# A fixed order for the entry of a fp32 decoder trunk, rotary tables under the value columns, and more raw rooms for the memory projection

## The chip, the cores and the metric

The kernel runs on one core of a Trainium2 chip. The metric is the device time of one launch in microseconds. Engines are named as in the profile: PE (TensorE, matrix products), PEld (its weight loads), DVE (VectorE), ACT (ScalarE), POOL (GpSimd) and SP (SyncE, which issues most DMAs).

## The reference

Two layers over 1024 rows of width 1024, all in fp32. Layer 0 is attention in three groups of dilated windows, layer 1 a gated linear recurrence; each also attends to 256 memory rows. Cut to layer 0, where the change lies:

```
h = rms_norm(x, norm_gain[0])
cols = h @ w_in_a                      # 1024 x 11264: q, k, v of 3 groups, memory queries, gate
q, k = rms_norm(q, q_gain), rms_norm(k, k_gain)
q, k = apply_partial_rotary(q, cos, sin), apply_partial_rotary(k, cos, sin)   # first 32 of 128 columns of a head
mix  = dilated window attention of each group, merged by softmax denominators
kv   = rms_norm(mem, mem_gain) @ w_kv                 # for both layers
mem_out = softmax(rms_norm(q_mem) @ km.T) @ vm
y    = concat(mix, mem_out) * silu(gate)
x    = x + y @ w_out
```

`cos` and `sin` are tables of `positions * inv_freq`, 1024 rows by 16 frequencies.

## The kernel before

A product in fp32 is made of three matmuls: each operand is split into a high part and a low part (`hi`, `lo`; ACT copies the high part, DVE or POOL subtracts it), and hi x hi, hi x lo and lo x hi are added in PSUM. Weights come by DMA as raw pieces of 512 KB ("raw" rooms in SBUF), and ACT and DVE split them into `wh` and `wl` (four of each).

The program of layer 0, in order of time:

1. **The entry.** Eight row tiles of x (128 rows each) are loaded, normalized (ACT squares and sums a row, DVE and POOL make the inverse root `rv`, `rr`, DVE scales `xt`), turned by eight PE transposes a tile (`pt`, L857) and split into `hhi` and `hlo`. The tiles come in pairs, j and j + 4. Of each pair three block sums (`s2`, `s3`, `s4`, and `s1` in place) are made for the next stage. Under it runs the projection of the first 512 gate columns: per tile 8 x 3 matmuls (L286 to L288), 192 in all, then tanh, a product and a write to `gate_scr`. POOL also makes the rotary tables here. A scheduler sets the order of the instructions on each engine by its own costs.
2. **The column groups.** Nine groups of 1024 columns (q, k or v of one window group) by Strassen's seven products, so 28 steps of twelve matmuls a group (`step`, L995 to L997), in the order keys, values, queries for group 2. Queries and keys are normalized and rotated (POOL) and turned. Here the order on each engine is pinned as written.
3. **The memory part.** Keys and values of the memory for both layers (`mem_part`), with the raw pieces loaded into two rooms in turn (L198), then the 512 memory query columns (L1291 to L1293) and the attention to the memory. Keys are turned and written ("spilled") some steps after their product, from a list `later`, one entry at each query tile.
4. Attention of the three groups, output projection, layer 1.

`pinned(...)` adds ordering dependencies, so that an engine executes in the written order; without engines named it holds for PE alone.

Of the kernel before, what the change touches and what calls it, by code (L numbers as in the profile page):

```python
# [24 lines left out]
I32 = mybir.dt.int32  # L25
# [78 lines left out]
def trunk_kernel(ctx, tc, x, mem, pos, norm_gain, w_in_a, q_gain_a, k_gain_a, qk_gain_t, w_out_a,  # L104
# [89 lines left out]

    def piece_raw(src):

        raw = rpool.tile([128, 1024], F32, name="raw")
        WQ.dma_start(raw[:].rearrange("p (a b) -> p a b", a=src.shape[1]), src)  # L198
        return raw
# [459 lines left out]
    plan_chunk(("gate", 0), w_in_a, GATE_A)  # L659
# [108 lines left out]
    with ExitStack() as sa:  # L768
# [29 lines left out]
        def tables():  # L798

            posi = wx.tile([128, NT], I32, name="m2")  # L800
            Y.dma_start(posi[:], pos[:, 0:NT])
            flat = room("m3").rearrange("p h d -> p (h d)")
            n_ = NT * 16
            v3 = lambda o: flat[:, o:o + n_].rearrange("p (a b) -> p a b", b=16)
            ang, kk, tmp = v3(0), v3(n_), v3(2 * n_)
            inv, posf = flat[:, 3 * n_:3 * n_ + 16], flat[:, 3 * n_ + 16:3 * n_ + 16 + NT]
            G.tensor_copy(posf, posi[:])
            Y.dma_start(inv, cst[:, C_IF:C_IF + 16])
            n3 = [128, NT, 16]
            G.tensor_tensor(ang, bc(posf[:, :, None], n3), bc(inv[:, None, :], n3), op=OP.mult)  # L810
# [7 lines left out]
            for big in (4096.0, 1.0):  # L818
                G.tensor_scalar(kk, ang, 1.0 / (2.0 * math.pi * big), magic, op0=OP.mult, op1=OP.add)
                G.tensor_scalar(kk, kk, -magic, None, op0=OP.add)  # L820
                for c in parts:
                    G.tensor_scalar(tmp, kk, -c * big, None, op0=OP.mult)
                    G.tensor_tensor(ang, ang, tmp, op=OP.add)
            G.tensor_scalar(ang, ang, 3.1415925, -3.1415925, op0=OP.min, op1=OP.max)
            A.activation(sn, ang, AF.Sin)
            A.activation(cs, ang, AF.Sin, scale=0.5)
            G.tensor_tensor(cs, cs, cs, op=OP.mult)
            G.tensor_scalar(cs, cs, -2.0, 1.0, op0=OP.mult, op1=OP.add)
            for i, gn in enumerate((q_gain_a, k_gain_a)):
                Y.dma_start(gr[:, i], bass.AP(tensor=gn.tensor, offset=gn.offset, ap=[[0, 128], [HD, NG], [1, ROT]]))  # L830
            gt = wx.tile([128, 2 * NG], F32, name="m2")
            Y.dma_start(gt[:], qk_gain_t)
            V.tensor_tensor(gqk, gt[:, :NG], gt[:, NG:], op=OP.mult)
            V.memset(gqk[0:ROT, :], 1.0)
# [5 lines left out]
        s1raw = {}  # L840

        def x_pair(j):

            t_, r = {}, {}
            for half in range(2):
                m = j + 4 * half
                xt = ipool.tile([128, D], F32, name="xt", bufs=2)
                first = Y.dma_start(xt[:], tile_of(x, m))
                if m == 0:
                    with tc.issue_after(first.ins):  # L850
                        row_bcast(gain[:], norm_gain[0], D)
                        Y.dma_start(ident[:], cst[:, C_ID:C_ID + 128])
                norm_rows(xt[:], gain[:], D, ipool, bufs=1, inplace=True)
                for kh in range(2):
                    t = pT.tile([128, 4, 128], F32, name="pt")
                    for b in range(4):
                        T.transpose(t[:, b, :], xt[:, (4 * kh + b) * 128:(4 * kh + b + 1) * 128], ident[:])  # L857
                    hi, lo = (hts[n][:, 4 * kh:4 * kh + 4, m * 128:(m + 1) * 128] for n in ("hi", "lo"))
                    split_evac(hi, lo, t[:])
                    if (half, kh) != (1, 1):  # L860
                        r[half, kh] = ipool.tile([128, 4, 128], F32, name=f"r{half}{kh}")[:]
                        copy(A, r[half, kh], t[:])
                    else:
                        s1raw[j] = room(f"m{j}")
                        V.tensor_tensor(s1raw[j], r[1, 0], t[:], op=OP.add)
                if half:
                    for i, n in enumerate(("hi", "lo")):
                        Y.dma_start(a21_scr[i][:, :, j * 128:(j + 1) * 128], hts[n][:, 0:4, m * 128:(m + 1) * 128].bitcast(F32))
            at = slice(j * 128, (j + 1) * 128)

            def keep(s, src):
                copy(A, sums[s, "hi"][:, :, at], src)
                G.tensor_tensor(sums[s, "lo"][:, :, at], src, sums[s, "hi"][:, :, at].bitcast(F32), op=OP.subtract)

            c3 = room(f"u{j % 2}")
            V.tensor_tensor(c3, r[0, 0], r[1, 0], op=OP.subtract)
            keep("s3", c3)
            c2 = room(f"w{j % 2}")
            V.tensor_tensor(c2, s1raw[j], r[0, 0], op=OP.subtract)
            keep("s2", c2)  # L880
            c4 = room(f"u{(j + 1) % 2}")
            V.tensor_tensor(c4, r[0, 1], c2, op=OP.subtract)
            keep("s4", c4)
# [192 lines left out]
        def step(k, fill=None):  # L1076
# [771 lines left out]
```

## Time and profile before

| | |
|---|---|
| median of 3 runs | 2092.5 us (2089.14 to 2092.95) |
| the profiled execution | 2096.68 us |
| its span | 2094.8 us, granted clock 0.994 |
| PE busy | 2051.2 us, 98% |
| DVE, ACT, POOL busy | 58%, 41%, 26% |
| entry (0 to the first matmul of L995) | 80.75 us |
| DMA | 277.22 MB, mean 132 GB/s |

The span runs from the first to the last instruction of one profiled execution. "Busy" of PE counts pipelined matmuls whose ends are modelled. A row of the timeline has its start, its duration, engine, line, operation and tiles (out<-in), shape and type, count, and in brackets the idle time of the engine before it and what ended it.

### The profile page before, as it was taken

The numbers are of one execution on the slowest core, as the hardware profiler recorded it, in microseconds if no ns is written. First come the engines' busy times: TensorE is split into PE (matmuls) and PEld (weight loads), VectorE is DVE, ScalarE is ACT, GpSimd is POOL, SyncE is SP. The second block draws the span as 40 slices with busy tenths as digits, with TensorE's granted clock in tenths as the row PEclk, the third lists the DMA queues.
The fourth block names the chain that finished last, engine by engine and source line by source line (L and its number), as shares of the span: only waits on it lengthen the run. The fifth ranks groups of instructions, "written<-read, shape, count | busy, mean of one in ns | idle before, by whom it ended". The sixth has DMA issues, their size and how long they took to land.

```text
span 2094.8 us, 29661 instructions
## 1 busy us (share of the span) xinstructions
PE 2051.2 (98%) x10713; PEld 1732.8 (83%) x10713; DVE 1220.6 (58%) x2452; ACT 860.8 (41%) x1635; POOL 553.1 (26%) x701
## 2 busy tenths in 40 slices
PE   6999999999999999999899999999999999999999
PEld 5788888888888888788788888888888888888887
DVE  5665467746757357555567454425477663776443
ACT  6454355633654245446667332224432222222220
POOL 7363066703746036121123200013100000000221
PEclk9999999999999999999999999999999999999999
DMA  6368469553553425517998474331201211213642
GB/s 204 101 122 120 130 126 110 126 147 97 126 136 113 159 81 189 173 31 271 307 314 288 146 263 148 123 90 46 76 28 60 65 51 41 61 51 96 236 131 110
DMA packets 418898, 277.22 MB, mean 132 GB/s; under 512 B 220593, under 2 KB 344769, under 8 KB 416705
## 3 DMA queue, kind: packets, MB, share of 16 engines
q1 hardware_dynamic: 402096, 252.26, 43.7%
q10 hardware_dynamic: 16656, 23.07, 3.0%
q8 instruction: 85, 1.39, 0.3%
q14 instruction: 61, 0.49, 0.1%
HBM read 192.32 MB, written 82.97 MB: 131 GB/s over the span
## 4 chain that ended last, share of the span: by engine, by line
PE 51%; DMA 2%; ACT 0%; DVE 0%; issue 0%; POOL 0%; SPq 0%; ACTq 0%; DVEq 0%
PE acc L527 5%; PE acc L528 5%; PE acc L529 5%; PE acc L633 4%; PE acc L634 4%; PE acc L635 4%; PE acc L286 3%; PE acc L288 3%; PE acc L287 3%; PE s L1350 2%; PE s L1603 1%; PE pt L1603 1%; PE po L1377 1%; PE pt L1364 1%; PE acc L1377 1%; DMA o_scr<-os 1%
## 5 line engine op out<-in xcount | busy, mean ns | idle before, releaser
L172 ACT ACTIVATE wh<-raw 128x1024 fp32r<-128x1024 f32 x202 | 212.4, 1054 | 176.6 <-PE acc L528 48.7
L181 POOL TENSOR_TENSOR rr<-rv,nhalf 128x4 f32<-128x4 f32 (+1 forms) x54 | 49.9, 924 | 755.0 <-DVE rv L179 747.8
L1040 POOL TENSOR_TENSOR rr<-rv,nhalf 128x4 f32<-128x4 f32 x96 | 122.7, 1279 | 390.7 <-DVE rv L1038 389.9
L928 DVE TENSOR_TENSOR wl<-raw,wh 128x1024 fp32r<-128x1024 f32 x122 | 152.8, 1253 | 112.3 <-ACT wh L172 111.8
L529 PE MATMUL acc<-hhi,wl 128*128 128x512 f32 x448 | 178.7, 399 | 0.0
L528 PE MATMUL acc<-hlo,wh 128*128 128x512 f32 x448 | 178.5, 398 | 0.0
L527 PE MATMUL acc<-hhi,wh 128*128 128x512 f32 x448 | 177.6, 396 | 0.0
L230 DVE TENSOR_TENSOR wl<-raw,wh 128x1024 fp32r<-128x1024 f32 x80 | 101.2, 1269 | 121.7 <-ACT wh L172 119.1
L633 PE MATMUL acc<-wh,yhi 128*128 128x512 f32 x360 | 142.7, 398 | 0.5 <-ACT yhi L172 0.5
L634 PE MATMUL acc<-wl,yhi 128*128 128x512 f32 x360 | 141.0, 392 | 0.0
L635 PE MATMUL acc<-wh,ylo 128*128 128x512 f32 x360 | 139.8, 393 | 0.0
L286 PE MATMUL acc<-wh,hhi 128*128 128x512 f32 x320 | 126.5, 401 | 8.2 <-ACT hhi L172 7.1
L287 PE MATMUL acc<-wl,hhi 128*128 128x512 f32 x320 | 127.0, 398 | 1.7 <-DVE wl L230 1.7
L995 PE MATMUL acc<-wh,hhi 128*128 128x512 f32 x324 | 127.6, 394 | 0.0
L996 PE MATMUL acc<-wl,hhi 128*128 128x512 f32 x324 | 126.2, 390 | 1.2 <-DVE wl L928 1.2
L288 PE MATMUL acc<-wh,hlo 128*128 128x512 f32 x320 | 126.9, 399 | 0.5 <-DVE hlo L307 0.4
L997 PE MATMUL acc<-wh,hlo 128*128 128x512 f32 x324 | 126.3, 390 | 0.0
L1355 ACT ACTIVATE pa<-pa,st 128x128 f32<-128x128 f32 (+1 forms) x192 | 84.5, 442 | 44.8 <-DVE st L1353 44.6
L528 PEld LDWEIGHTS acc<-hlo,wh 128*128 128x128 f32 x448 | 84.3, 188 | 15.7
L527 PEld LDWEIGHTS acc<-hhi,wh 128*128 128x128 f32 x448 | 84.2, 188 | 15.6
L529 PEld LDWEIGHTS acc<-hhi,wl 128*128 128x128 f32 x448 | 84.3, 188 | 15.4
L932 DVE TENSOR_TENSOR raw<-raw 128x1024 f32<-128x1024 f32 x68 | 85.3, 1261 | 16.9 <-DMA raw<-in_w_in_a_dram 16.8
(360 smaller groups left out, 5280.6 us busy)
## 6 DMA issues: line engine op xcount, KB each, us to landing
raw<-in_w_in_a_dram SPq DMA_DIRECT2D x113, 512.0 KB, 4.5
raw<-in_w_in_b_dram SPq DMA_DIRECT2D x40, 512.0 KB, 3.8
qk_scr<-m SPq DMA_DIRECT2D x48, 256.0 KB, 3.7
o_scr<-os SPq DMA_DIRECT2D x96, 128.0 KB, 4.7
raw<-in_w_mem_kv_dram SPq DMA_DIRECT2D x16, 512.0 KB, 3.9
kT<-qk_scr SPq DMA_DIRECT2D x8, 1024.0 KB, 6.3
qT<-qk_scr SPq DMA_DIRECT2D x8, 1024.0 KB, 9.2
vv<-v_scr SPq DMA_DIRECT2D x8, 1024.0 KB, 7.7
```

Of the source, the lines that this page charges most:

```text
L172: A.activation(dst, src, AF.Copy)
L286: T.matmul(ps, hi, wh[:, j, :], start=at == 0, stop=False)
L287: T.matmul(ps, hi, wl[:, j, :], start=False, stop=False)
L288: T.matmul(ps, lo, wh[:, j, :], start=False, stop=at == n - 1)
L527: T.matmul(ps[:], wh[:, k, :], mh, start=k == 0, stop=False)
L528: T.matmul(ps[:], wh[:, k, :], ml, start=False, stop=False)
L529: T.matmul(ps[:], wl[:, k, :], mh, start=False, stop=k == 7)
L633: T.matmul(pss[ch][:], hi[:, k, :], wh[:, j, :], start=first and k == 0, stop=False)
L634: T.matmul(pss[ch][:], hi[:, k, :], wl[:, j, :], start=False, stop=False)
L635: T.matmul(pss[ch][:], lo[:, k, :], wh[:, j, :], start=False, stop=end and k == 3)
L928: V.tensor_tensor(lo[:], source(n, h), hi.bitcast(F32), op=OP.subtract)
L995: T.matmul(flat, hi, wh, start=kt == 0 and p in (0, 1, 5), stop=False, **on)
```

## The change

Four edits go together.

*The entry in written order.* `x_pair` is taken apart into small functions (load, square, scale, turn, evacuate high, keep, low, sums, splits), and their calls are written out in one order inside `pinned(PE, DVE, Activation, Pool)`. The gate product is cut into parts `gate_mm(t, i)`: six matmuls of row tile t with weight piece i. The first weight piece is loaded ahead of the second row tile, all four pieces ahead of the third; two of them go to rooms `u23` and `w23` in place of the two raw rooms. Row tiles have three rooms instead of two. The eight transposes of the next pair's tiles stand among the gate parts of the present pair. Gate writes are issued by SP instead of ACT.

On PE, from the second pair on. Before (`pt` are the transposes, `acc` the gate matmuls), the rows around a turn:

```order
L286 MATMUL acc<-wh,hhi 128x512
L287 MATMUL acc<-wl,hhi 128x512
L288 MATMUL acc<-wh,hlo 128x512
L857 MATMUL pt<-ident,xt 128x128 x8
L286 MATMUL acc<-wh,hhi 128x512
L287 MATMUL acc<-wl,hhi 128x512
L288 MATMUL acc<-wh,hlo 128x512
```

After, at the same place (the second pair's first tile ends, and `po` is its second tile):

```order
L1141 MATMUL po<-wh,hhi 128x512
L1142 MATMUL po<-wl,hhi 128x512
L1143 MATMUL po<-wh,hlo 128x512
L868 MATMUL pt<-ident,xt 128x128 x8
L1141 MATMUL po<-wh,hhi 128x512
L1142 MATMUL po<-wl,hhi 128x512
```

The rows look alike, but their tiles differ: before, the matmuls behind the transposes are the gate product of the tiles just turned; now they are the rest of the pair that was turned earlier, 30 matmuls of a pair ahead of its successor's first transposes or between its two tiles, and 18 behind them.

*Tables as DVE steps.* `tables()` on POOL becomes `table_steps()`, a generator on DVE of which one step runs at each of the column steps k = 4 and on, and `table_ends()` behind it. For group 2 the order becomes values, keys, queries, so that the tables are not needed in the first group.

On POOL, from the second row tile on (`rr` is the root that the scale of a row tile waits for, `m` the tables, `s3lo` and so on low parts of the sums). Before:

```order
L181 TENSOR_TENSOR rr_181<-rv_179,nhalf 128x1
L807 CAST m_242<-m_240 128x8
L810 TENSOR_TENSOR m_242<-m_242 128x128
L819 TENSOR_SCALAR m_242<-m_242 128x128
L820 TENSOR_SCALAR m_242<-m_242 128x128
L822 TENSOR_SCALAR m_242<-m_242 128x128
L823 TENSOR_TENSOR m_242<-m_242 128x128
```

After:

```order
L181 TENSOR_TENSOR rr_197<-rv_195,nhalf 128x1
L181 TENSOR_TENSOR rr_272<-rv_270,nhalf 128x1
L181 TENSOR_TENSOR rr_278<-rv_276,nhalf 128x1
L903 TENSOR_TENSOR s3lo<-u_280,s3hi 128x4x128
L903 TENSOR_TENSOR s2lo<-w_282,s2hi 128x4x128
L903 TENSOR_TENSOR s4lo<-u_289,s4hi 128x4x128
```

The tables' operations have left POOL's entry; roots and low parts follow each other.

*More raw rooms.* While the memory's products are under way, `piece_raw` takes four rooms in turn: the two raw rooms, `u23` and `w23`. On SP, where the memory weights are loaded (`mgt` are small gains, `gatem_scr` a gate write, `qk_scr` writes of queries and keys). Before:

```order
L198 DMA raw<-in_w_mem_kv_dram 128x2x512
L1066 DMA qk_scr_92<-u_6673 128x4x128
L198 DMA raw<-in_w_mem_kv_dram 128x2x512 x9
L198 DMA raw<-in_w_in_a_dram 128x2x512 x4
L1259 DMA kv_scr<-os 128x512
```

After:

```order
L202 DMA raw<-in_w_mem_kv_dram 128x2x512
L1080 DMA qk_scr_92<-u_6649 128x4x128
L202 DMA raw<-in_w_mem_kv_dram 128x2x512
L202 DMA u_7497<-in_w_mem_kv_dram 128x2x512
L202 DMA raw<-in_w_mem_kv_dram 128x2x512 x3
L202 DMA u_7592<-in_w_mem_kv_dram 128x2x512
L202 DMA w_7621<-in_w_mem_kv_dram 128x2x512
L202 DMA raw<-in_w_mem_kv_dram 128x2x512
L202 DMA raw<-in_w_in_a_dram 128x2x512
```

One load into `w` (of the piece behind `u_7497`) has moved ahead of all rows shown here.

*A spill earlier.* At query tile 0 two entries of `later` run instead of one.

```
+    own_raw = lambda: rpool.tile([128, 1024], F32, name="raw")
+    more_raws = [own_raw]
     def piece_raw(src):
-        raw = rpool.tile([128, 1024], F32, name="raw")
+        more_raws.append(more_raws.pop(0))
+        raw = more_raws[-1]()
...
-            G.tensor_tensor(ang, bc(posf[:, :, None], n3), bc(inv[:, None, :], n3), op=OP.mult)
+            V.tensor_copy(posf, posi)
+            V.tensor_tensor(sn, bc(posf[:, :, None], n3), bc(inv[:, None, :], n3), op=OP.mult)
+            yield
...
-                for c in parts:
-                    G.tensor_scalar(tmp, kk, -c * big, None, op0=OP.mult)
-                    G.tensor_tensor(ang, ang, tmp, op=OP.add)
+                for at, c in enumerate(parts):
+                    V.scalar_tensor_tensor(sn, cs, -c * big, sn, op0=OP.mult, op1=OP.add)
+                    if at % 3 == 2:
+                        yield
...
-        groups = [(i, g) for g in (2, 1, 0) for i in (1, 2, 0)]
+        groups = [(i, g) for g in (2, 1, 0) for i in ((2, 1, 0) if g == 2 else (1, 2, 0))]
...
+                if 3 < k < 26:
+                    if next(tables, tables) is tables and made_tables:
+                        made_tables.pop()()
...
+        def gate_mm(t, i):
+            if t not in gates:
+                gate_room(t)
+            wh, wl = W[i]
+            for j in range(2):
+                k = 2 * i + j
+                hi, lo = lhs_natural(tiles[t])(k)
+                T.matmul(gates[t], hi, wh[:, j, :], start=k == 0, stop=False)
+                T.matmul(gates[t], hi, wl[:, j, :], start=False, stop=False)
+                T.matmul(gates[t], lo, wh[:, j, :], start=False, stop=k == 7)
...
+        with pinned(E.PE, E.DVE, E.Activation, E.Pool):
...
+            for j in range(4):
+                a, b = 2 * j, 2 * j + 1
+                a_, b_ = (a + 2, b + 2) if j < 3 else (None, None)
+                order = [(b, 1), (b, 2), (b, 3)] if j == 0 else [(a, 0), (a, 1), (b, 0), (b, 1), (a, 2), (b, 2), (a, 3), (b, 3)]
+                mm = iter(order)
+                more_mm = lambda: gate_mm(*next(mm))
+                if j:
+                    more_mm()
+                    if a_:
+                        x_scale(a_)
+                    for t in (a - 2, a - 1):
+                        gate_end(t)
...
+                if a_:
+                    if j:
+                        more_mm()
+                    x_scale(b_)
+                    for kh in range(2):
+                        x_turn(a_, kh)
+                    more_mm()
+                    for kh in range(2):
+                        x_high(a_, kh)
+                        x_keep(a_, kh)
+                        x_low(a_, kh)
+                    x_load(a_ + 2)
+                if j:
+                    more_mm()
...
+                if a_:
+                    for kh in range(2):
+                        x_turn(b_, kh)
+                    more_mm()
...
+                more_raws[:] = [own_raw] * 2 + [lambda n=n: wx.tile([128, 1024], F32, name=n) for n in ("u23", "w23")]
                 with pinned():
                     for _ in ahead_of:
                         pass
+                more_raws[:] = [own_raw]
...
+                    if m == 0:
+                        later.pop(0)()
                     half_step(0)
```

More of the change, by code (lines that the diff above doesn't have):

```diff
@@ L657, in plan_slices @@
             plan_slice(("gate_m", i), w_in_a, GATE_A + 1024 + i * 128)
-    plan_chunk(("gate", 0), w_in_a, GATE_A)
     plan_slices(MG0[:1])
@@ L839, in trunk_kernel @@
         gain = ipool.tile([128, D], F32, name="gain")
[L840 to L883, printed above, removed]
@@ L885, in keep_s1, with x_load @@
-        def keep_s1(j):
-            hi, lo = (operand("s1", n)[:, :, j * 128:(j + 1) * 128] for n in ("hi", "lo"))
-            copy(A, hi, s1raw[j])
-            G.tensor_tensor(lo, s1raw[j], hi.bitcast(F32), op=OP.subtract)
-        groups = [(i, g) for g in (2, 1, 0) for i in (1, 2, 0)]
+        s1raw, xt, rr, r, turned_x = {}, {}, {}, {}, {}
+        tiles = [j + 4 * half for j in range(4) for half in range(2)]
+        def x_load(t):
+            if t < NT:
+                xt[t] = ipool.tile([128, D], F32, name="xt", bufs=3)
+                return Y.dma_start(xt[t][:], tile_of(x, tiles[t]))
@@ new lines, in x_square, with x_scale @@
+        def x_square(t):
+            ss = small.tile([128, 1], F32, name="ss1")
+            m = tiles[t]
+            A.activation(hts["lo"][:, :, m * 128:(m + 1) * 128], xt[t][:].rearrange("p (k c) -> p k c", k=8), AF.Square,
+                         accum_out=ss[:])
+            rr[t] = rsqrt(ss[:], 1, D)
+        def x_scale(t, parts=1):
+            w = D // parts
+            for c in (slice(i * w, (i + 1) * w) for i in range(parts)):
+                V.scalar_tensor_tensor(xt[t][:, c], xt[t][:, c], rr[t][:], gain[:, c], op0=OP.mult, op1=OP.mult)
@@ new lines, in x_turn, with x_room, x_high, x_keep @@
+        def x_turn(t, kh):
+            turned_x[t, kh] = p = pT.tile([128, 4, 128], F32, name="pt")
+            for b in range(4):
+                T.transpose(p[:, b, :], xt[t][:, (4 * kh + b) * 128:(4 * kh + b + 1) * 128], ident[:])
+        def x_room(n, t, kh):
+            return hts[n][:, 4 * kh:4 * kh + 4, tiles[t] * 128:(tiles[t] + 1) * 128]
+        def x_high(t, kh):
+            copy(A, x_room("hi", t, kh), turned_x[t, kh][:])
+        def x_keep(t, kh):
+            if (t % 2, kh) != (1, 1):
+                r[t, kh] = ipool.tile([128, 4, 128], F32, name=f"r{t % 2}{kh}")[:]
+                copy(A, r[t, kh], turned_x[t, kh][:])
@@ L1073, in trunk_kernel @@
         LAST = 28 * len(groups) - 1
+        made_tables = [table_ends]
         sums_at = {}
@@ L1092, in step @@
             flip(k - BEHIND)
[L1094 to L1114 removed]
+        wraws, W, gates = {}, {}, {}
```

183 lines of the change are left out of this document (141 added, 42 removed).

## The prediction

> **What bounds the kernel now.** I read the head of the page first, then busy time in windows, then the list of TensorE's waits in the first 120 us, and last the timeline where it waits.
>
> ```profile
> span 2094.8 us, 29661 instructions
> PE 2051.2 (98%) x10713; PEld 1732.8 (83%) x10713; DVE 1220.6 (58%) x2452; ACT 860.8 (41%) x1635; POOL 553.1 (26%) x701
> ```
>
> TensorE is busy 2051.2 of 2094.8 us, so a change in order can win only the 43.6 us in which it is idle, and what it loses at half clock. Windows show where that is (columns after the window: its length, then busy us of PE, PEld, DVE, ACT, POOL, each with its instructions; granted clock; DMA share; GB/s).
>
> ```profile
> 0.00:10.00 10.00, 1.97 (x8) 1.57 (x8) 1.68 (x5) 4.02 (x7) 0.94 (x6) 1.00 0.82 265
> 10.00:20.00 10.00, 7.80 (x28) 6.09 (x29) 7.81 (x12) 7.62 (x13) 8.32 (x14) 1.00 1.00 307
> ...
> 40.00:50.00 10.00, 6.00 (x29) 4.65 (x28) 5.99 (x9) 8.03 (x14) 9.40 (x12) 0.89 0.43 146
> 50.00:60.00 10.00, 9.98 (x37) 7.61 (x37) 3.64 (x6) 4.25 (x8) 2.57 (x5) 0.77 0.18 45
> ...
> 80.70:157.00 76.30, 75.12 (x347) 61.83 (x347) 54.18 (x74) 38.66 (x52) 42.58 (x59) 1.00 0.57 115
> 157.00:233.00 76.00, 76.00 (x352) 62.83 (x351) 37.98 (x43) 34.40 (x42) 16.85 (x25) 1.00 0.82 147
> ...
> 872.98:891.00 18.02, 14.25 (x58) 10.69 (x56) 5.39 (x8) 5.54 (x8) 1.01 (x1) 0.90 0.51 150
> sum 80.75, PE 61.02 PEld 47.69 DVE 46.30 ACT 46.55 POOL 50.12; mean PE 7.63 PEld 5.96 DVE 5.79 ACT 5.82 POOL 6.27
> ```
>
> The last row sums the entry, 0 to 80.75 us (its end is the first matmul of the column groups, shown below): TensorE is idle for 80.75 - 61.02 = 19.7 us of it, and part of the rest runs at a lower clock (0.77 in 50 to 60). From there the groups are full (76.00 of 76.00). The stretch at the end of the memory part loses 3.8 us. The change works on these two places.
>
> ```profile
> PE pt L857 <- DVE xt L321: 8.2, 2, 8.0
> PE acc L286 <- ACT hhi L172: 7.1, 3, 4.0
> PE acc L996 <- DVE wl L928: 1.2, 1, 1.2
> ...
> 35.30 1.03 PE L857 MATMUL pt<-ident,xt 128*128 128x128 f32 x8
> 38.15 0.50 PE L286 MATMUL acc<-wh,hhi 128*128 128x512 f32 x1 [1.81 <-ACT hhi L172]
> 44.11 1.04 PE L857 MATMUL pt<-ident,xt 128*128 128x128 f32 x8
> 49.15 0.79 PE L286 MATMUL acc<-wh,hhi 128*128 128x512 f32 x1 [4.00 <-ACT hhi L172]
> 50.16 0.63 PE L288 MATMUL acc<-wh,hlo 128*128 128x512 f32 x1
> 50.59 0.63 PE L286 MATMUL acc<-wh,hhi 128*128 128x512 f32 x1
> 80.53 0.39 PE L288 MATMUL acc<-wh,hlo 128*128 128x512 f32 x1
> 80.75 0.39 PE L995 MATMUL acc<-wh,hhi 128*128 128x512 f32 x1
> ```
>
> Before, the eight transposes of a row tile (L857) stand after the gate matmuls of an earlier pair, and the next gate matmul waits until that tile is turned and split: 1.81 and 4.00 us with nothing else to run. A matmul starts 0.22 us after the one ahead of it at full clock (80.53 to 80.75, 0.227 on average) and 0.43 us at half clock (50.16 to 50.59).
>
> **The change, part by part.** Durations of the entry's pieces, by group:
>
> ```profile
> L321 DVE SCALAR_TENSOR_TENSOR xt<-xt,rr,gain 128x1024 f32<-128x1024 f32 x8 | 12.4, 1552 | 10.6 <-POOL rr L181 9.4 <-DMA gain<-in_norm_gain_dram 1.2
> L307 DVE TENSOR_TENSOR hlo<-pt,hhi 128x512 fp32r<-128x512 f32 x16 | 10.6, 683 | 8.9 <-ACT hhi L172 8.9
> L172 ACT ACTIVATE hhi<-pt 128x512 fp32r<-128x512 f32 x16 | 9.0, 591 | 8.8 <-PE pt L857 8.8
> L873 POOL TENSOR_TENSOR s2lo<-w,s2hi 128x512 fp32r<-128x512 f32 x4 | 5.6, 1399 | 0.0
> L822 POOL TENSOR_SCALAR m<-m 128x128 f32<-128x128 f32 x14 | 11.3, 811 | 1.2
> L823 POOL TENSOR_TENSOR m<-m 128x128 f32<-128x128 f32 x14 | 7.9, 561 | 1.0
> 6.68 1.28 DVE L321 SCALAR_TENSOR_TENSOR xt<-xt,rr,gain 128x1024 f32<-128x1024 f32 x1 [1.24 <-DMA gain<-in_norm_gain_dram]
> 12.23 1.21 DVE L230 TENSOR_TENSOR wl<-raw,wh 128x1024 fp32r<-128x1024 f32 x1
> raw<-in_w_in_a_dram SPq DMA_DIRECT2D x1, 512.0 KB, 3.7
> ```
>
> *Work of TensorE.* Unchanged: 192 gate matmuls x 0.227 = 43.5 us and 16 groups of four transposes. A group of four in a running stream costs about 0.36 us (eight take 1.03 with their tail), so 5.8 us. With the start at about 7.4 us the entry cannot end before 56.7.
>
> *The first 29 us (tiles 0 and 1).* These stay bound by DVE and ACT, not by TensorE. I add up the DVE chain. The first scale starts at 6.68 as now, but in halves, so the transposes start at 7.4. The first weight piece now stands third among the 512 KB loads, right behind the gain, which landed at 6.6 (that row's wait); at the 307 GB/s of 10 to 20 us it lands 1.7 later, at 8.3. Its high part (ACT) is ready at 9.4. DVE then does one low part (1.21) and two splits (0.6 each back to back, 683 ns alone), to 11.9; tile 1's scale waits for square and root until 12.6 and ends at 13.9; then three low parts, two splits and one sum (5.4, with 0.7 of waits) to 20.0; two sums, two scales and one sum (4.5) to 24.5. The turned tile 3 needs its PSUM room emptied by ACT (five evacuations of 0.5 back to back from 23.9), so its last transposes run at 26.3, and twelve matmuls later, at 29.3, pair 1 begins.
>
> *The rest.* Three pairs x 48 x 0.227 = 32.6 us and eight groups of transposes = 2.9 us. In a pair DVE needs 8.9 us (4 splits, 3 + 1 sums, 2 scales, 2 gate products, by the rows above), ACT 9.2, POOL 6.7 (four low parts of 1.4 and two roots), all under TensorE's 12.3. The longest chain from a pair's last gate matmul to its successor's second scaled tile is tanh, gate product, three sums and a scale, about 5.0 us; 30 matmuls and the first tile's eight transposes (7.5 us) stand ahead of that tile's transposes now. So TensorE runs through: 29.3 + 35.5 = 64.8. I add 0.8 for DVE beside POOL (the scale's mean is 1552 ns against 1.28 us for the first) and 1.4 for one spell of seven matmuls at half clock, as explained below: the groups begin at **67.0** instead of 80.75, a gain of **13.75 us**. Bounds: 64.8, and 72 if TensorE stays at half clock to 30 us and waits once as long as before (4.0).
>
> *The first wait of the groups* (L996 on wl, 1.2 us) goes: the next weights are split when the sixth of eight gate parts runs. Gain **1.2**.
>
> *Tables.* 36 POOL operations (L822 and L823 alone 19.2 us) stood among the roots that the scales wait for (9.4 us of L321's idle time). They become some 25 DVE operations in steps 4 to 25 of the first group. That group is now the values, where DVE was busy 37.98 of 76.00 us and POOL 16.85. A DVE pass over 128x128 is not in the trace. Between a quarter of the 128x512 pass (0.17) and the whole (0.68) I take 0.3, nearer the quarter, as each waits for the one before: 7.5 us in all, at most 17. That is under the 38 free, so nothing. The cover gone, it would be 7.5. Two of the three table loads of ACT in the entry leave, off the path.
>
> *Order of the groups.* Values first; then keys, queries and the next keys stand in a row, three groups that keep DVE at 54.18 of 76.30. TensorE lost only the 1.2 us above in that heaviest group, so I take nothing; bounds 0 and 2 us lost.
>
> *Gate writes* move from ACT's queue to SP's: on SP, only pair 3's last input load is behind them, which has 5 us to spare.
>
> *Memory part.*
>
> ```profile
> SPq L198 <- DVE wl L227: 20.9, 8, 4.9
> ...
> 877.57 1.06 ACT L172 ACTIVATE wh<-raw 128x1024 fp32r<-128x1024 f32 x1 [2.04 <-DMA raw<-in_w_in_a_dram]
> 886.22 0.69 ACT L1253 ACTIVATE os<-pt,mgk 128x512 f32<-128x512 f32 x1 [6.01 <-PE pt L346]
> kv_scr<-os SPq DMA_DIRECT2D x1, 256.0 KB, 3.9
> ...
> 872.98 0.39 PE L1291 MATMUL acc<-wh,hhi 128*128 128x512 f32 x1
> 878.68 0.49 PE L1291 MATMUL acc<-wh,hhi 128*128 128x512 f32 x1 [0.91 <-ACT wh L172]
> 879.94 0.50 PE L1292 MATMUL acc<-wl,hhi 128*128 128x512 f32 x1 [0.77 <-DVE wl L230]
> 881.27 0.63 PE L1293 MATMUL acc<-wh,hlo 128*128 128x512 f32 x1
> 881.70 0.63 PE L1291 MATMUL acc<-wh,hhi 128*128 128x512 f32 x1
> 891.00 1.09 PE L346 MATMUL pt<-ident,qn 128*128 128x128 f32 x4 [2.10 <-DVE rv L179]
> ```
>
> With two raw rooms a load is issued when DVE has done the piece two before it; it then takes 3.7 us to land, so a piece comes every 3.1 us while TensorE uses one in 12 x 0.227 = 2.7. By the query columns the lead is used up (0.91 + 0.77). Four rooms take the loads off that ring, from some 6 us earlier; the new wait is that the loads into u and w stand on SP behind the landing of the last query and key writes, which still leaves them ahead of their use. Then the second wait: ACT stood 6.01 us at the second key spill (L1253), whose transposes come under query tile 1, with the square of query tile 0 queued behind. Both spills now come under tile 0. ACT's chain there is two spills that wait for value writes of 3.9 us each, then square, reduce, root, scale: I get 883.2 for the scaled tile against 884.6 when TensorE reaches it. From 872.98 to 891.00 stand 48 matmuls and two groups of transposes: 10.9 + 0.7 = 11.6 instead of 18.0, **6.4 us**, and the slow spell that follows (891 to 894) goes, some 1.5: **7.9**. Bounds 3 (only the loads help) and 8.
>
> *The clock, weighed.* Half-clock matmuls follow the gaps of 4.00 us (49.15), of 0.91 and 0.77 (881.27 to 881.70), and of 2.10; none follows 1.81. So in this trace gaps of one to two microseconds cost a spell in about half the cases, and I charge one. The Trainium skill, "TensorE: Matmul & The Clock Gate", section "What's actually happening", says that the array falls to half rate only after an idle window of about 3.4 us. By that rule the entry would end 1.4 us earlier and the sum be 24.3; the row at 881.70 disagrees, as its gaps are shorter.
>
> *Sum.* 13.75 + 1.2 + 7.9 = **22.9 us**. The profiled execution took 2096.68 us with 2094.8 of span; it is 4.2 above the median of the three runs, 2092.5. From the median: 2092.5 - 22.9 = **2070**.
>
> **The rivals.** *Cold entry.* Until 26 us TensorE's work is broken by DVE's. If it runs at half clock that long, 30 matmuls cost 0.2 more each, of which the gaps take up about half: the groups begin at 70 and the time is 2073. For it: the first matmuls at half clock now; against: full rate was reached by 17 us with gaps after that. Chance 0.15. The Trainium skill, in the section named above, asks for a busy window of some 3.4 us before full rate, which speaks for this case.
>
> *The memory part gives 0 to 3.* SP holds the loads, or the spills' value writes land late and ACT holds the square as before. For it: the margin of 1.4 us. Then 13.75 + 1.2 + 0 to 3: 2075 to 2077.5. Chance 0.15.
>
> *Half the entry.* The chain of 5.0 us is longer than its cover, as DVE passes beside POOL take up to twice as long. PE waits 2 to 3 us in each pair: 2078. Chance 0.08.
>
> *Slower.* All four engines now run one written order in the entry; one late piece holds everything behind it. If the ring PE, ACT, DVE does not overlap, a pair costs up to 12.3 + 8.9 + 9.2 us. It decides when TensorE waits (22.9 + 4.2) / 3 = 9 us in each of three pairs; before, the longest such wait was 4.00. Time 2097 or more, chance 0.03.
>
> *No change*: the gain is given back at a stage that DMA bounds. Later loads are issued from TensorE's progress, not from a fixed time, so I give it 0.02.
>
> **How the numbers follow.** The forecast holds 0.57 by itself (2066 to 2074). 0.2% is 4.2 us, about what can be told from no change. Faster 0.95, same 0.02, slower 0.03. The range runs from 2062 (the entry at its lower bound, 2.2 us better, the runs' own spread of 3.4 below the median, and 2 for what I did not see) to 2080, which takes in the rivals but the last two.
>
> **What would show it.** Right: the first group's matmul near 67 us; no wait of TensorE above 1.5 us between 30 us and there; transposes of tiles 2 to 7 inside a stream; no waits on wh, wl or rv at the query columns; POOL almost idle in the first group and DVE under 55 us in it. Wrong: waits of a gate matmul on hhi in each pair; TensorE waiting at the table steps or in the third heavy group; SP standing before a load into u or w while TensorE waits for wl.

## The result, and the profile after

The changed kernel takes 2078.17 us in the median of six runs (2073.70 to 2080.30), against 2091.92 for the kernel before on the same chip (six runs, 2088.98 to 2092.95). The ratio is 0.9936, 95% interval 0.9923 to 0.9949: 13.75 us faster, where 22.9 were forecast.

The profiled execution after took 2080.30 us, that of before 2096.68, so the two traces differ by 16.4. They lie 2.1 and 4.8 us above the medians, and this alone is 2.6 of the 16.4. The head of the page after:

```profile
span 2078.5 us, 29644 instructions
PE 2045.1 (98%) x10713; PEld 1729.6 (83%) x10713; DVE 1228.0 (59%) x2476; ACT 858.5 (41%) x1635; POOL 532.1 (26%) x664
```

The windows of the entry (columns as before: length, busy us of PE, PEld, DVE, ACT and POOL, clock, DMA share, GB/s):

```profile
0.00:10.00 10.00, 2.15 (x9) 1.75 (x9) 2.34 (x6) 4.21 (x6) 0.76 (x5) 1.00 0.83 269
10.00:20.00 10.00, 9.37 (x30) 6.83 (x31) 8.43 (x12) 8.98 (x15) 0.61 (x2) 1.00 0.95 293
20.00:30.00 10.00, 7.47 (x36) 5.73 (x35) 8.70 (x10) 5.97 (x11) 7.28 (x5) 0.89 0.84 306
30.00:40.00 10.00, 10.00 (x47) 8.29 (x46) 9.27 (x13) 6.98 (x14) 6.82 (x5) 0.94 0.54 175
40.00:50.00 10.00, 10.00 (x53) 8.37 (x52) 7.85 (x13) 6.58 (x13) 5.81 (x6) 1.00 0.38 132
```

The list of TensorE's waits up to the groups (us in total, times, longest), and the groups' first matmul in the timeline:

```profile
PE pt L868 <- DVE xt L863: 8.6, 3, 7.4
PE pt L868 <- DVE hlo L882: 2.0, 1, 2.0
PE acc L1141 <- ACT hhi L172: 0.4, 1, 0.4
```

```profile
68.88 0.39 PE L1009 MATMUL acc<-wh,hhi 128*128 128x512 f32 x1
```

After the first 8 us there is one wait worth the name, 2.0 us, and from 30 us on TensorE is full. The groups begin at 68.88 instead of 80.75. Windows of the changed kernel: the first group with the first 12 us of the second (which begins at 145.04), the memory part, the query columns, attention as a whole and its first 60 us.

```profile
68.88:157.00 88.12, 88.12 (x390) 72.99 (x389) 48.56 (x70) 30.77 (x42) 1.29 (x1) 1.00 0.38 126
814.80:860.77 45.97, 45.97 (x216) 37.99 (x214) 30.38 (x50) 26.71 (x45) 5.82 (x4) 1.00 0.67 212
860.77:919.22 58.45, 58.45 (x319) 49.80 (x317) 27.96 (x60) 23.52 (x59) 15.20 (x15) 1.00 0.15 45
954.74:1193.99 239.25, 227.02 (x1522) 203.83 (x1520) 140.33 (x631) 140.46 (x488) 52.89 (x48) 0.99 0.83 271
954.74:1014.74 60.00, 57.74 (x420) 52.72 (x419) 36.53 (x176) 41.70 (x157) 0.00 (x0) 1.00 1.01 348
```

The last four of these in the kernel before:

```profile
827.44:872.98 45.54, 45.54 (x212) 37.69 (x210) 29.13 (x49) 25.56 (x42) 4.47 (x4) 1.00 0.59 184
872.98:939.46 66.48, 62.71 (x321) 52.35 (x319) 30.01 (x62) 25.21 (x61) 15.20 (x15) 0.95 0.19 57
973.27:1210.67 237.40, 226.27 (x1521) 204.01 (x1520) 140.27 (x631) 141.99 (x488) 52.89 (x48) 0.99 0.83 274
973.27:1033.27 60.00, 57.65 (x419) 52.63 (x418) 36.61 (x174) 41.83 (x157) 0.00 (x0) 1.00 1.00 349
```

The window limits are TensorE's first instructions of the stages, so the table below is read from them and from the same first instructions of the stages between (positive is earlier after):

| from before to after | us |
|---|---|
| entry: 80.75 to 68.88 | +11.87 |
| groups: the first wait, 1.2 us and its tail, gone | +1.49 |
| end of the groups and the memory part | -1.15 |
| query columns: 66.48 to 58.45 | +8.03 |
| rest of memory attention | -1.71 |
| attention: 237.40 to 239.25 | -1.85 |
| out projection of the first half | -0.67 |
| all that follows | +0.03 |
| sum, at the last matmul | +16.04 |

So 21.4 us are won at the two places of the change, and 5.4 are given back, 4.2 of them in stages whose code is the same. That loss, and the 1.9 us missing in the entry, are what the experiments are about. In attention the sixteen DMA engines are full for the first 60 us in both kernels (shares 1.00 and 1.01). TensorE's longest wait comes behind that, 4.85 us at 73.6 us from the start of the stage: it waits for a copy into `os`, and the copies wait until an earlier `os` has landed. From the list of waits in attention after:

```profile
PE po L1530 <- ACT os L172: 5.8, 2, 4.9
...
ACT os L172 <- DMA o_scr<-os: 9.8, 5, 2.9
```

### The profile page after: what moved, and what is told of

The parts are those of the page before. It is cut to its first block, busy times and chain, and to the rows that moved or that the text cites. A ratio compares the mean times of both kernels' runs of the same rounds, so it can differ in the third digit from the quotient of the medians.

```text
span 2078.5 us, 29644 instructions
## 1 busy us (share of the span) xinstructions
PE 2045.1 (98%) x10713; PEld 1729.6 (83%) x10713; DVE 1228.0 (59%) x2476; ACT 858.5 (41%) x1635; POOL 532.1 (26%) x664
## 3 DMA queue, kind: packets, MB, share of 16 engines
q8 instruction: 85, 1.39, 0.3%
## 4 chain that ended last, share of the span: by engine, by line
PE 48%; DMA 3%; DVE 1%; ACT 0%; issue 0%; POOL 0%; SPq 0%; DVEq 0%; ACTq 0%
PE acc L532 5%; PE acc L531 5%; PE acc L533 5%; PE acc L637 4%; PE acc L639 4%; PE acc L638 4%; PE acc L292 3%; PE acc L291 3%; PE acc L290 3%; PE s L1503 2%; PE s L1756 2%; PE pt L1756 2%; PE po L1530 1%; PE pt L1517 1%; PE acc L1530 1%; DMA qT<-qk_scr 1%
## 5 line engine op out<-in xcount | busy, mean ns | idle before, releaser
L172 ACT ACTIVATE wh<-raw 128x1024 fp32r<-128x1024 f32 x198 | 208.1, 1054 | 167.0 <-PE acc L532 49.0
L942 DVE TENSOR_TENSOR wl<-raw,wh 128x1024 fp32r<-128x1024 f32 x122 | 153.0, 1255 | 105.1 <-ACT wh L172 104.6
L234 DVE TENSOR_TENSOR wl<-raw,wh 128x1024 fp32r<-128x1024 f32 x74 | 92.6, 1255 | 117.6 <-ACT wh L172 115.2
L1009 PE MATMUL acc<-wh,hhi 128*128 128x512 f32 x324 | 127.5, 394 | 0.0
L1011 PE MATMUL acc<-wh,hlo 128*128 128x512 f32 x324 | 126.4, 390 | 0.0
L1010 PE MATMUL acc<-wl,hhi 128*128 128x512 f32 x324 | 126.2, 389 | 0.0
L1508 ACT ACTIVATE pa<-pa,st 128x128 f32<-128x128 f32 (+1 forms) x192 | 84.6, 442 | 51.3 <-DVE st L1506 49.5
L291 PE MATMUL acc<-wl,hhi 128*128 128x512 f32 x256 | 99.9, 390 | 0.0
L292 PE MATMUL acc<-wh,hlo 128*128 128x512 f32 x256 | 99.5, 390 | 0.0
L290 PE MATMUL acc<-wh,hhi 128*128 128x512 f32 x256 | 98.9, 391 | 0.0
L946 DVE TENSOR_TENSOR raw<-raw 128x1024 f32<-128x1024 f32 x68 | 85.2, 1261 | 13.5 <-DMA raw<-in_w_in_a_dram 13.5
```

What stands on the lines that cost most here:

```text
L172: A.activation(dst, src, AF.Copy)
L290: T.matmul(ps, hi, wh[:, j, :], start=at == 0, stop=False)
L291: T.matmul(ps, hi, wl[:, j, :], start=False, stop=False)
L292: T.matmul(ps, lo, wh[:, j, :], start=False, stop=at == n - 1)
L942: V.tensor_tensor(lo[:], source(n, h), hi.bitcast(F32), op=OP.subtract)
L1009: T.matmul(flat, hi, wh, start=kt == 0 and p in (0, 1, 5), stop=False, **on)
```

## The experiments

Medians are beside the kernel before on the same chip. A ratio of five runs is uncertain by about 0.0013, so two of them differ surely only beyond about 0.0018, 4 us.

**Each half of the change alone.** `e_entry` takes the memory edit out of the changed kernel:

```diff
-                more_raws[:] = [own_raw] * 2 + [lambda n=n: wx.tile(...) for n in ("u23", "w23")]
...
-                    if m == 0:
-                        later.pop(0)()
```

> The changed kernel without the memory part's edit: loads of pieces use two raw rooms again, and both key spills come where they came before. In the two traces the groups begin 11.9 us earlier, their first wait of 1.5 us is gone, and the memory part with its query columns gains 8.0, together 21.4 us; the medians show 13.75. So some 5 to 8 us come back later, in code that the change does not touch. Theory A, the loss goes with the memory edit (attention starts sooner after it and waits more): this kernel gains 12 to 13.5 us, 2078.5 to 2080. Theory B, the loss goes with the entry's shift: it gains 6 to 8 us, 2084 to 2086. Theory C, the loss is spread over all that follows in proportion: it gains 8.5 to 9.5 us, 2082.5 to 2083.5. The old waits on wh, wl and rv at the query columns should stand again, 3 to 4 us.

`e_memory` puts these lines (and the rotation in `piece_raw`) into the kernel before.

> The kernel before with the memory part's edit alone: four raw rooms for the loads while the memory part ends, and both key spills under the first query tile. By the two traces that part and the query columns gain 8.0 us. Theory A, the later loss goes with this edit: 0 to 2 us of it are left, 2090 to 2092. Theory B, it goes with the entry: 8 us, 2084. Theory C, in proportion: 5 us, 2087.

Measured: the entry alone 2082.21 against 2093.65, ratio 0.9943 (0.9929 to 0.9957), 11.4 us by the medians and 11.9 by the ratio (9.0 to 14.9); the memory edit alone 2093.27, ratio 0.9997 (0.9988 to 1.0006): between 1.3 us lost and 2.5 won. Theory A, the loss goes with the memory edit, fits both best, though the entry stays just under its 12 to 13.5; B's 8 us and C's 5 for the memory edit lie outside the interval. Yet the edit does at its place what it should. The window of the query columns with the entry alone:

```profile
860.71:926.48 65.77, 61.66 (x321) 51.04 (x319) 30.36 (x62) 25.89 (x62) 15.22 (x15) 0.97 0.21 64
```

TensorE's waits in that window, those that the edit is to remove:

```profile
PE pt L350 <- DVE rv L179: 2.1, 1, 2.1
PE acc L1441 <- DVE wl L234: 1.6, 3, 0.8
PE acc L1440 <- ACT wh L172: 0.4, 1, 0.4
```

With the memory edit alone, windows of the query columns and of the memory part ahead of them:

```profile
875.62:934.07 58.45, 58.45 (x319) 49.80 (x317) 27.99 (x60) 23.55 (x59) 15.22 (x15) 1.00 0.15 45
827.34:875.62 48.28, 46.89 (x216) 37.76 (x213) 30.48 (x50) 26.62 (x45) 5.38 (x4) 1.00 0.68 202
```

65.77 us against 58.45. In the second kernel 2.7 go at once, since the memory part took 48.28 instead of 45.54 with 1.39 us of waits. The end of the query columns is 5.4 us earlier than before, the last matmul of that trace 2.6, and the medians show 0.4.

Two of the smaller losses in the table go with the entry, not with the memory edit. Where the last group's columns are turned, ahead of the window of the memory part, TensorE waits 1.51 us for ScalarE's `w` (L1078) with the entry alone and 1.39 in the changed kernel, against 0.31 before and with the memory edit alone. The rest of memory attention is 1.0 us longer with the entry alone, and with the memory edit alone as long as before.

**The changed kernel again, and time put in by hand.** `e_after` is the changed kernel unaltered.

> The changed kernel again, for a second trace of it and for times beside the three others. The memory part's edit gained 8.0 us up to the end of the query columns in the changed kernel's trace and 5.4 in its trace alone, but alone the medians show 0.4 of 2093.65. In the six traces so far the attention stage, whose code is the same in all, loses 7.5 to 13.9 us to idle TensorE. Theory A, that idle time differs by chance from one execution to the next: this trace has another amount than the 12.2 us of the first, by 2 us or more. Theory B, it is set by the kernel: 12.2 again, within 1. The median should be near 0.9936 of the kernel before.

`e_pad` lets TensorE do idle work ahead of the first query tile:

```diff
                     if m == 0:
+                        pad = pT.tile([128, 4, 128], F32, name="pt")
+                        for b in range(88):
+                            T.transpose(pad[:, b % 4, :], ident[:], ident[:])
```

> The changed kernel with 88 transposes of the identity, whose result nobody reads, on TensorE ahead of the first query tile: some 8 us of lost time at the place where the memory part's edit gained 8. Theory A, what is gained or lost ahead of attention goes through to the end: it is 8 us slower than the changed kernel, 2086 to 2088. Theory B, attention makes most of it up, because its transfers then have that time as a lead: it is 0 to 3 us slower, 2078 to 2081, and its trace shows less idle time in attention, 5 to 7 us instead of 12.2.

Measured: 2079.11 for the changed kernel against 2091.34, ratio 0.9941 (0.9928 to 0.9953), and 2085.30 with the pad, ratio 0.9972 (0.9963 to 0.9981). Windows of the memory part with the pad, and of attention behind it:

```profile
815.52:871.10 55.58, 55.58 (x303) 47.61 (x302) 31.91 (x51) 28.44 (x46) 4.48 (x4) 1.00 0.61 192
964.11:1199.25 235.14, 225.97 (x1522) 204.12 (x1520) 138.97 (x632) 141.27 (x488) 52.90 (x48) 0.99 0.83 275
```

Attention in the second trace of the changed kernel:

```profile
955.56:1193.93 238.37, 225.83 (x1521) 202.64 (x1520) 138.86 (x631) 140.89 (x488) 52.85 (x48) 1.00 0.83 272
```

The pad costs 9.6 us where it stands (45.97 to 55.58) and 6.2 at the end; attention behind it idles 9.2 us (235.14 - 225.97), against 12.2 and 12.5 in the two traces of the changed kernel. By the ratios the pad costs 6.5 us, with an interval of about 3 to 10. So theory B's 0 to 3 is unlikely; that all 9.6 go through is not excluded, and that a part comes back is likely, not shown. In the test of chance theory B holds by its own terms, 12.5 us against 12.2, but the parts of the sum did not repeat (the longest wait was 4.85 us in one trace and 2.36 in the other). Nor is the sum that firm: in `e_poollater`, `e_fill2` and `e_fill`, further below, where attention and the memory edit are the same, it is 10.4, 11.4 and 13.9 us.

**The two parts of the memory edit.** `e_noraws` leaves out the line on `more_raws`, `e_nopop` the two on `later`.

> The changed kernel without the four raw rooms: the loads of the memory part's and the query columns' pieces use two rooms again. In the trace with the entry alone TensorE waited 0.44 + 1.57 us for pieces at the query columns and 2.10 for the root, and the columns took 65.8 us against 58.5. Theory A, time lost there goes through to the end: some 4 us come back, 2082. Theory B, attention makes it up: within 1.5 us of the changed kernel.

> The changed kernel with both key spills where they came before (one under each of the first two query tiles) and the four raw rooms kept. Theory A: the wait of 2.10 us for the root and its half-clock spell come back, some 3.5 us, 2081.5. Theory B: attention makes it up, within 1.5 us of the changed kernel.

Measured: 2081.27, ratio 0.9952 (0.9938 to 0.9966), and 2079.07, ratio 0.9943 (0.9930 to 0.9955), beside 0.9941 for the whole: 2.2 us slower than the whole and equal to it, by the medians. The intervals overlap, so neither verdict stands. At the place itself the parts are plain: the query columns take 60.82 us without the rooms and 61.08 without the moved spill, 58.45 with both, 65.77 with neither. Each part alone wins 4.7 to 5.0 of the 7.3.

**Attention's queue.** In `e_act` the writes of `spill` go by ScalarE's queue; `e_entry_act` is the same without the memory edit.

```diff
-                    Y.dma_start(group_rows(o_scr[g][hp // 2], g, m - 1 + i)...
+                    A.dma_start(group_rows(o_scr[g][hp // 2], g, m - 1 + i)...
```

> The changed kernel with the attention results of the second and third reach (two 128 KB writes behind each copy of os) issued on ScalarE's queue instead of SyncE's, where they stand behind head loads of 1 MB. In all traces TensorE's longest wait in attention is at 70 to 74 us from its start, for ScalarE's copy into os, which waits until an earlier os has landed. Theory A, attention is paced by that one queue: the wait of 2.2 to 5.9 us and those after it shrink, idle time in attention falls from 12.2 to 4 to 7 us, and the kernel is 4 to 7 us faster than the changed one, 2072 to 2075. Theory B, the bytes of the 16 DMA engines decide, which are full there on any queue: no change, 2078 to 2080.

> The same move of the attention writes in the kernel with the changed entry and the old memory part. Against the run beside it, it differs by the memory part's edit alone, which by the traces gains 7.3 us up to the end of the query columns but 0.5 to 1.5 in the medians. Theory A, what attention's queue gives and takes hides that gain: with the writes on the other queue 5 to 8 us of it come through, this kernel takes 5 to 8 us more than the run beside it. Theory B, the loss is elsewhere or stays: 0 to 2 us more.

Measured: 2087.43 against 2092.88, ratio 0.9976 (0.9966 to 0.9985), and 2091.53, ratio 0.9992 (0.9983 to 1.0001). The first misses both theories: 7.3 to 8.4 us slower than the changed kernel, by the two ratios measured for that one. The window of attention in `e_act`:

```profile
954.00:1203.45 249.45, 232.38 (x1521) 207.63 (x1520) 143.37 (x632) 141.37 (x488) 53.06 (x48) 0.97 0.79 260
```

The waits of TensorE and of ScalarE in it, and the place of the longest in ScalarE's timeline:

```profile
PE pt L1517 <- ACT pa L1508: 12.7, 8, 5.3
PE po L1530 <- ACT os L172: 3.0, 2, 2.0
...
ACT pa L1508 <- DMA raw<-in_w_in_a_dram: 6.1, 1, 6.1
ACT pa L1508 <- DMA kT<-qk_scr: 4.3, 2, 2.3
...
973.98 0.83 ACTq L1550 DMA_DIRECT2D o_scr<-os  x2
974.86 0.40 ACT L1508 ACTIVATE pa<-pa,st 128x128 f32<-128x128 f32 x1 [6.06 <-DMA raw<-in_w_in_a_dram]
```

The exponentials (`pa`, L1508) use neither a piece `raw` nor `kT`. They stand behind a write whose issue waits for an older transfer to land: the two writes at 973.98 are issued 0.07 us after a piece `raw` landed (973.91), and ScalarE has been idle until then. So the queue's wait moved onto ScalarE, ahead of what TensorE needs next: TensorE waits 12.7 us for exponentials, against 2.0 in the changed kernel. The 64 issues themselves also stand in ScalarE's order, 0.41 us each and 26.5 in all; no run parts this cost from the waits. With the writes there the memory edit is worth 0.0016, 3.3 us with an interval of about 0.6 to 6.0 (4.1 by the medians): between theories A and B, nearer to A's 5 than it was on SyncE's queue.

`e_rooms` leaves the queue alone and gives the copies one more room:

```diff
-            spool = s1.enter_context(tc.tile_pool(name="spill", bufs=3, ...
+            spool = s1.enter_context(tc.tile_pool(name="spill", bufs=4, ...
-                p = ap_.tile([128, 2, 256], F32, name="pa", bufs=4)
+                p = ap_.tile([128, 2, 256], F32, name="pa", bufs=3)
```

> The changed kernel with a fourth os room in attention, its memory taken from the pa rooms (three instead of four). Theory A: TensorE's waits in attention come from ScalarE's copy into os, which waits for an earlier os to land behind the head loads; one room more gives it a third more time, the wait at 70 to 74 us falls under 1 us, idle time there falls from 12.2 to 8 to 10, and the kernel is 2 to 4 us faster, 2075 to 2077. Rival: the pa room becomes the wait, or the backlog only grows until the fourth room is full too: 2078 to 2081.

Measured: 2077.89 against 2091.33, ratio 0.9939 (0.9925 to 0.9953): no change. The wait named in theory A is gone and another stands in its place. TensorE's and ScalarE's rows in attention:

```profile
PE po L1530 <- DVE os L1582: 6.6, 3, 5.1
...
ACT os L172 <- DMA o_scr<-os: 0.4, 1, 0.4
```

ScalarE waits 0.4 us for landed rooms instead of 9.8 and 7.1 in the two traces of the changed kernel, and TensorE then waits 5.1 at the merge of the first reach (L1582). Idle time fell to 8.65 us, as A had it, without effect on the median. Attention took 233.71 us in this trace, 4.7 to 5.5 less than in those two; but this execution lies 1.6 us below its kernel's median, and those lie 2.1 and 1.1 above theirs.

**The entry.** Pair 1's first gate matmul comes at 32.57 us, where the prediction had 29.3. What stood between, in the timeline of VectorE, POOL and TensorE (start, duration, in brackets the wait ahead):

```profile
21.30 1.27 DVE L863 SCALAR_TENSOR_TENSOR xt<-xt,rr,gain 128x1024 f32<-128x1024 f32 x1
22.50 1.76 DVE L897 TENSOR_TENSOR u<-r,w 128x512 f32<-128x512 f32 x1
24.18 2.31 DVE L863 SCALAR_TENSOR_TENSOR xt<-xt,rr,gain 128x1024 f32<-128x1024 f32 x1
26.41 1.27 DVE L882 TENSOR_TENSOR hlo<-pt,hhi 128x512 fp32r<-128x512 f32 x2
...
21.52 2.18 POOL L903 TENSOR_TENSOR s3lo<-u,s3hi 128x512 fp32r<-128x512 f32 x1 [0.34 <-ACT s3hi L172]
23.67 1.73 POOL L903 TENSOR_TENSOR s2lo<-w,s2hi 128x512 fp32r<-128x512 f32 x1
25.37 2.25 POOL L903 TENSOR_TENSOR s4lo<-u,s4hi 128x512 fp32r<-128x512 f32 x1
...
27.14 1.71 PE L868 MATMUL pt<-ident,xt 128*128 128x128 f32 x8 [1.96 <-DVE hlo L882]
28.51 0.78 PE L1141 MATMUL acc<-wh,hhi 128*128 128x512 f32 x1
29.08 0.63 PE L1142 MATMUL acc<-wl,hhi 128*128 128x512 f32 x1
29.51 0.63 PE L1143 MATMUL acc<-wh,hlo 128*128 128x512 f32 x1
```

The sum and the scale take their usual time and, with it, the rest of the POOL pass that had begun: 24.18 + 2.31 = 26.49 is 1.1 us after s2lo ended at 25.40. And s4lo, begun at 25.37, ends 1.1 us after that scale. The Trainium skill, "SBUF — State Buffer", section "Who interferes with whom", says that a VectorE instruction with two inputs in SBUF and a GpSimd one that reads SBUF share a port by an exclusive lock, held for the whole instruction. The trace agrees, with spans that are rough by 0.2 us. The two splits at 26.41, with one input in PSUM, ran beside s4lo and kept their 0.68 us each. Scales of 2.31 us stand in pairs 1 and 2 too (at 37.05 and 49.78), but there TensorE had gate matmuls enough and did not wait.

Three kernels test what that costs. `e_poollater` only issues POOL's three instructions of pair 0 later in the program; `e_fill` puts the third sum and the second scale of pair 0 ahead of its splits, and one gate part ahead of the next transposes; `e_fill2` does so in all pairs:

```diff
                 x_sum(j, "s3")
                 x_sum(j, "s2")
-                x_split(j, "s3")
-                x_split(j, "s2")
...
                 x_sum(j, "s4")
-                x_split(j, "s4")
...
                     for kh in range(2):
                         x_high(a_, kh)
                         x_keep(a_, kh)
                         x_low(a_, kh)
                     x_load(a_ + 2)
+                    for s in ("s3", "s2", "s4"):
+                        x_split(j, s)
-                if j:
-                    more_mm()
+                more_mm()
```

> The changed kernel with one order changed on one engine: POOL's three low parts of pair 0's sums (s3, s2, s4) stand behind the splits of row tile 2 instead of ahead of the last scale. In the changed kernel's trace the scale of tile 3 took 2.31 us beside POOL against 1.27 alone, the third sum 1.76 against 0.68, and TensorE then waited 1.96 us for a free transpose room and ran six matmuls at half clock. Theory: POOL and VectorE passes with both inputs in SBUF do not overlap, so the scale falls back to 1.3 and the sum to 0.7, tile 2's first split starts 1 to 2 us earlier, the wait shrinks to 0.3 or less, and pair 1 begins at 30 to 31 us instead of 32.6: 1.5 to 2.5 us faster than the changed kernel, 2075.5 to 2076.7. Rival: the durations are those of the operations themselves (their data comes late, or ScalarE's order holds the split); then nothing moves, 2078.

> The changed kernel with pair 0 written anew: the third sum and the scale of tile 3 stand ahead of all three splits (ScalarE and POOL) of pair 0's sums, which come behind tile 2's, and one more gate part (6 matmuls, 1.36 us) runs ahead of tile 3's transposes. Theory: tile 2's transposes are emptied from 23.6 us on instead of 24.8, tile 3's transposes find their room free, no half-clock spell follows, and pair 1 begins near 29 us instead of 32.6, where the prediction had it (29.3): 3 to 3.8 us faster than the changed kernel, 2074 to 2075. Rival: the late splits of pair 0 hold up ScalarE or the rooms of pair 1, and TensorE waits there instead: 0 to 1 us, 2077 to 2078.

> The changed kernel with the order of e_fill in all pairs: the third sum and the scale of the second tile stand ahead of the splits of the pair's sums, which come behind the first tile's. In e_fill pair 0 went as expected (its scale 1.28 us, its sum 0.69, no wait, pair 1 begun some 3 us earlier), but pair 1 then had the old pattern (scale 2.31 us beside POOL, TensorE waiting 2.00 for a room, a half-clock spell) and the groups began at 68.87, as without it. Theory: DVE passes that meet a POOL pass set the entry's pace in whichever pair has them; with all pairs in the new order no wait over 0.7 us is left after 23 us and the groups begin at 65 to 66.5: 2 to 3 us faster than the changed kernel, 2076 to 2077. Rival: the wait moves on once more, to a later pair or to the roots behind POOL's splits, and the groups begin at 68 to 69: no change, 2079.

`e_poollater`: 2079.22 against 2093.65, ratio 0.9932 (0.9918 to 0.9945). Its trace has the same spans (scale 2.31, wait 1.96, groups at 69.01), because POOL had nothing between the old place and the new one: a later place in the program delays nothing on an idle engine. It tests nothing.

`e_fill`: 2077.37, ratio 0.9927 (0.9914 to 0.9939). Pair 0 went as expected, and the pattern stood again in pair 1. Its timeline, on VectorE, POOL and TensorE:

```profile
35.67 2.31 DVE L863 SCALAR_TENSOR_TENSOR xt<-xt,rr,gain 128x1024 f32<-128x1024 f32 x1
...
36.86 2.25 POOL L903 TENSOR_TENSOR s2lo<-w,s2hi 128x512 fp32r<-128x512 f32 x1
...
38.63 1.71 PE L868 MATMUL pt<-ident,xt 128*128 128x128 f32 x8 [2.00 <-DVE hlo L882]
```

The groups began at 68.87, 0.01 us earlier. `e_fill2`: 2074.76 against 2091.33, ratio 0.9922 (0.9907 to 0.9936). The scales of the entry as a group, in the changed kernel:

```profile
L863 DVE SCALAR_TENSOR_TENSOR xt<-xt,rr,gain 128x1024 f32<-128x1024 f32 x7 | 12.1, 1722 | 0.7 <-POOL rr L181 0.7
```

And in `e_fill2`:

```profile
L863 DVE SCALAR_TENSOR_TENSOR xt<-xt,rr,gain 128x1024 f32<-128x1024 f32 x7 | 9.0, 1281 | 0.7 <-POOL rr L181 0.7
```

Its list of TensorE's waits in the entry, and the groups' first matmul in its timeline:

```profile
PE pt L868 <- DVE xt L863: 8.4, 3, 7.5
PE pt L868 <- DVE hlo L882: 1.0, 1, 1.0
```

```profile
66.36 0.39 PE L1009 MATMUL acc<-wh,hhi 128*128 128x512 f32 x1
```

With no scale behind POOL (1281 ns in the mean instead of 1722) the groups begin at 66.36, inside the 65 to 66.5 that the theory gave; of the two sub-claims, the one on waits is missed by 0.3 us. `e_fill2` differs from `e_fill` by the order in the pairs behind pair 0 alone, and between the two the groups' start moves from 68.87 to 66.36. The time lies below the 2076 to 2077 expected. This is the fastest median of all kernels here. Its lead over the changed kernel is 1.7 to 2.5 us by the groups' start (68.06 in that kernel's second trace) and 0.0014 to 0.0019 by the ratios, which overlap; as a faster kernel it is likely, not shown.

## Why the prediction was right, and where its sum was off

*Direction and time.* 2078.17 lies in the range of 2062 to 2080, near its end. The forecast itself, 2070, was 8 us too fast. That the range holds the time is in part luck: its upper end was drawn for rivals that did not happen, and what did happen to the memory term was given a chance of 0.02. That the whole change measured 13.75 us, the number that was forecast for the entry alone, is coincidence.

*Entry, 13.75 us forecast, 11.87 measured.* The first 29 us were said to be bound by VectorE and ScalarE, which held. From the second pair on no gate matmul waited on `hhi`, and from 32.57 to 68.88 TensorE ran through in 36.3 us, all at full clock, where 35.5 were worked out. The term that was too small is "0.8 for DVE beside POOL". The row that it was taken from, eight scales at 1552 ns against 1.28 us, already holds 2.2 us. In pair 0 alone two passes lost 1.1 (the sum) and 1.0 (the scale), so VectorE's chain ended at 26.49 where 24.5 was worked out. The split behind them kept the transposes waiting for 1.96, and a spell of six matmuls at half clock followed, which the prediction had charged further on: pair 1 began 3.3 us late. `e_fill2` shows the mechanism by taking it away. The rivals on the entry fell: TensorE was at full clock from 18 us to that spell, and no pair from the second on waited.

*The first wait of the groups*, 1.2, measured 1.49.

*Tables and order of the groups*, both at nothing: right. The 14 passes of the tables' main step took 290 ns each, as estimated (0.3), TensorE was full through the first group and 12 us beyond (88.12 of 88.12), with VectorE at 48.56 over that stretch, under the 55 named, and POOL at 1.29. The three heavy groups in a row cost nothing.

*Memory part, 7.9 us.* At the query columns 8.03 were measured, all three waits gone. The step that failed is the one behind it, that such a gain reaches the end. "No change: given back at a stage that DMA bounds" got 0.02, with the reason that later loads are issued from TensorE's progress. For this term alone that rival was the better one: the edit alone is worth at most 2.5 us in the runs. The rival whose time came nearest, "The memory part gives 0 to 3" (2075 to 2077.5), was not what happened: its reasons, held loads or late spills, would have cost the gain at its place.

Where the gain goes is settled in part. In the memory part itself, counted from its first product to the query columns, the edit alone takes 2.8 us more than the kernel before (64.28 against 61.50), and seven traces with both edits take 0.2 to 1.7 more than the entry alone (62.42); new waits are part of it, as one on `qn`, 0.8 to 0.9 us in two of these traces and in that of the edit alone. The rest goes behind the query columns, 6.0 us in attention between the traces of the entry alone and of the changed kernel, 1.5 in attention and 1.3 behind it between those of the kernel before and of the edit alone. Its cause stays open. That transfers set the pace there is argued, not shown: taking one wait away (`e_rooms`) left the median where it was, and a pad ahead of attention (`e_pad`) was perhaps made up in part. Where the same code with its writes on SyncE's queue and three `os` rooms follows the short query columns, attention takes 237.6 to 240.5 us (six traces). Where something was lost ahead of it (the kernel before, the entry alone, the pad) it takes 233.2 to 237.4, and with half of the memory edit 235.4 and 238.1. Part of this may be chance: the trace of 233.2 is of an execution 2.1 us below its kernel's median, those of 239.4 and 240.5 lie 4.2 and 4.0 above theirs. The transfers of attention's first 4 us are issued within 0.5 us of the same distances from its start in all of these traces, so no lead of the transfers was found that would explain the rest. One trace of most kernels cannot part a rule from chance.

*The clock, weighed.* The row at 28.51 bears on it again: half-clock matmuls, 0.43 us apart, behind a wait of 1.96 us. By the Trainium skill, "TensorE: Matmul & The Clock Gate", section "What's actually happening", that wait is too short for it; the charge of one spell was right. The wait of 0.95 in `e_fill2` was followed by none. The kernel before has one more such spell, which the prediction does not list: eight matmuls from 68.21 us on, 0.43 us apart, behind waits of 1.30 and 0.36 us. So gaps of one to two microseconds cost a spell there in three of four cases, not in about half.

## What to carry to other kernels

A gain is priced at the end of the program, not at its place: list the stages behind it in which DMA engines are full, and price the gain once as passed on and once as lost there. Where VectorE and POOL work on SBUF side by side, take the durations from rows in which they do, and move the pass that others wait for out of the other's way in every repetition of the pattern, since moving it in one only moves the wait to the next. An instruction issued later on an engine with nothing to do is not delayed, and a transfer issued from a busy engine can hold that engine until an older transfer lands.

## What the runs showed of the hardware

A VectorE pass with both inputs in SBUF and a POOL pass over 128x512 run one after the other: 2.31 us instead of 1.28 for the scale, 2.18 to 2.25 instead of 1.28 for POOL in pair 0. VectorE passes that read PSUM beside POOL kept their 0.68. A wait of 1.96 us was followed by six matmuls at half clock, one of 0.95 by none, and one of 1.81 in the kernel before by none. Issuing two 128 KB writes per copy from ScalarE cost 7 to 8 us; ScalarE waited up to 6.1 us there for another queue's transfer.
